# Strassen blocks of the last feed-forward layer: sums and the first two operand splits traced one block ahead; 24 general slots, 11 temporaries

## The chip, the cores and the metric

The kernel runs on one core of one Trainium2 chip. A core has TensorE (PE: matmuls, with the weight loads shown apart as PEld), VectorE (DVE), ScalarE (ACT), GpSimd (POOL) and SyncE (SP, which here only issues loads). The metric is the device time of one execution in microseconds (us). Lower is better. Before the change, three runs took 2473.5 to 2476.78 us, with a median of 2476.52.

## The reference

One inference step of a two-layer trunk on 512 prompt tokens and 8 sample tokens, 520 columns in all, with model width 1024. Each layer has two SwiGLU feed-forward blocks of inner width 2816; layer 0 has a gated MLP (gMLP) mixer, layer 1 an S5 state-space mixer; both have cross-attention into 256 memory tokens. The change touches the last feed-forward block of layer 1 alone (and two sizes that the whole program uses). What that block computes:

```python
def _swiglu(h, wg, wu, wd):
    return (jax.nn.silu(h @ wg) * (h @ wu)) @ wd
...
        x = x + 0.5 * _swiglu(_rmsnorm(x, norm_ffn2[i]), ffn2_wg[i], ffn2_wu[i], ffn2_wd[i])
    return _rmsnorm(x, norm_final), jnp.stack(new_re), jnp.stack(new_im), jnp.stack(new_v)
```

All of it is float32.

## The kernel before

Every float32 operand of a matmul is held as a high and a low half, and a product is three matmuls per 128 rows: high x high, high x low, low x high. A weight tile is split where it is used: ACT copies it to the reduced type (`wh`, L352), and VectorE subtracts that from the original (`wl`, L353). The pools of `wh` and of `wl` hold four tiles each (`WB = 4`), raw weights (`wr`) four (`WR = 4`).

The last feed-forward layer makes its 2816 hidden rows in 11 blocks of 256 columns of `wg` and `wu`. Blocks 0 and 1 are plain (`gu`). Blocks 2 to 10 go through `gu7`, which loads a block's weights as two tiles (`r1`, `r2`, four DMAs at L480) and runs `seven`: one level of a Strassen scheme, gate and up side by side. It splits the weights into quarters A11, A12, A21, A22 and the input into matching operands made once (`seven_x`: B11, B21, B22 and T4 lie in the tiles `xs`, T1 to T3 in `xt`). The seven products of a block and their weight operands, in the order of the program, are

- B11 with A11, then T2 with S2 = A21 + A22 - A11, then B21 with A12;
- T3 with S3 = A11 - A21, then T1 with S1 = A21 + A22;
- T4 with A22, then B22 with the second use of S2's tile, A12 - S2.

Each product is 24 matmuls of 260 columns (2 x 4 x 3). S1 and S2 are made by GpSimd (L368, L369), S3 and the second S2 by VectorE (L379, L380). The sums that combine products are VectorE's (L376 to L390, with one ACT copy at L374). Each of the four results goes through two scalings and a Silu (L485 to L487); when a hidden tile is complete it is split (L161 on ACT, L162 on VectorE).

After block 2, and then after each pair of blocks (3 and 4, 5 and 6, 7 and 8, 9 and 10), a down projection `down` takes four hidden tiles (192 matmuls) and adds to X (L500); the remaining two hidden tiles go through `last`. So blocks 4, 6, 8 and 10 follow directly on the block before them, and blocks 3, 5, 7 and 9 follow a down projection. "Odd" and "even" blocks below mean these.

S1, S2 and S3, hidden tiles, `xs`, `xt` and much else of the program are buffers of one size in one pool, the general slots (`SLOTS = 23`). Small float32 tiles of 520 columns (`t`: the sums e1 to e3, the block's halves of hidden rows, and in other stages the tiles of S5 and of its preparation) share a pool of 12.

What sets the order: the program is traced as Python, and when it is complete a planner of the framework lays down each engine's queue. It plays the program through once; of the instructions of an engine that are ready it takes the one traced first, and buffers of a pool are given out in the order in which their first writes were traced. On the chip the queues are fixed and each engine works through its own in order. Nothing in this layer is ordered by hand.

Of the kernel before, what the change touches and what calls it, by code (L numbers as in the profile page):

```python
# [9 lines left out]
F32 = mybir.dt.float32  # L10
F32R = mybir.dt.float32r
I32 = mybir.dt.int32
AF = mybir.ActivationFunctionType
# [10 lines left out]
DFF = 2816  # L24
# [5 lines left out]
KT = D // 128  # L30
NPAIR = 32
MAGIC = 12582912.0
SLOTS = 23
WB = 4
WR = 4
FFN_GROUPS = ((0, 6), (6, 12), (12, 18), (18, 22))
SEVEN_GROUPS = ((0, 4), (4, 8), (8, 12), (12, 16), (16, 20), (20, 22))
PLAIN = 2
BUFS = {"t": 12, "rs": 2, "rt": 4, "st": 10, "sti": 4, "mv": 4, "sc": 2, "cj": 2, "s5": 12, "s5i": 1,
        "s5r": 2}  # L40


class Prog:
    def __init__(self, ctx, tc, ins, outs, taps=None, stop=None):
# [4 lines left out]
        self.cp = ec(tc.tile_pool(name="cp", bufs=1))  # L49
        self.sp = ec(tc.tile_pool(name="sp", bufs=SLOTS))  # L50
        self.wp = ec(tc.tile_pool(name="wp", bufs=2))
# [15 lines left out]
    def tmp(self, shape=(128, NT), dt=F32, tag="t", name="t"):  # L67
        return self.tp.tile(list(shape), dt, name=self.nm(name), tag=tag, bufs=BUFS[tag])

    def ps(self):  # L70
        return self.pp.tile([128, 2, 512], F32, name=self.nm("ps"), tag="ps")
# [265 lines left out]

        return {"B11": B[0], "B21": B[2], "B22": B[3], "T1": T[0], "T2": T[1], "T3": T[2], "T4": B[1]}, last

    def seven(self, r1, r2, ops, ps):  # L340


        nc = self.nc
        V, G = nc.vector, nc.gpsimd
        sh = list(r1.shape[:3]) + [128]
        A11, A21, A12, A22 = r1[..., :128], r1[..., 128:], r2[..., :128], r2[..., 128:]
        n, nk = sh[1:3]

        def parts(src):
            hi = self.wp.tile(sh, F32R, name=self.nm("wh"), tag="wh", bufs=WB)  # L350
            lo = self.wp.tile(sh, F32R, name=self.nm("wl"), tag="wl", bufs=WB)
            nc.scalar.activation(hi, src, AF.Copy)  # L352
            V.tensor_sub(lo, src, hi.bitcast(F32))  # L353
            return hi, lo

        def product(p, w, b, first):

            hi, lo = w
            for x in range(n):
                for k in range(nk):  # L360
                    bh, bl = ops[b][k]
                    for i, (m, r) in enumerate(((hi, bh), (hi, bl), (lo, bh))):
                        self.mm(p[:, x, :HN], m[:, x, k], r, first and k == 0 and i == 0, k == nk - 1 and i == 2,
                                skip_group_check=not first)

        S1, S2, S3 = (self.slot(sh, F32, "S") for _ in range(3))
        w11 = parts(A11)
        G.tensor_add(S1, A21, A22)  # L368
        G.tensor_sub(S2, S1, A11)  # L369
        a, b, c = (ps() for _ in range(3))  # L370
        va, vb, vc = (p[:, :, :HN] for p in (a, b, c))
        e1, e2, e3 = (self.tmp([128, 2, HN]) for _ in range(3))
        product(a, w11, "B11", True)
        nc.scalar.copy(e1, va)  # L374
        product(b, parts(S2), "T2", True)
        V.tensor_add(e2, vb, e1)  # L376
        product(a, parts(A12), "B21", False)
        yield "11", va
        V.tensor_sub(S3, A11, A21)  # L379
        V.tensor_sub(S2, A12, S2)  # L380
        product(b, parts(S3), "T3", False)
        V.tensor_add(e3, vb, e1)
        product(c, parts(S1), "T1", True)
        V.tensor_add(e3, vc, e3)
        yield "22", e3
        product(b, parts(A22), "T4", False)
        V.tensor_add(e1, vb, e1)
        yield "21", e1
        product(c, parts(S2), "B22", False)
        V.tensor_add(e2, vc, e2)  # L390
        yield "12", e2


    def ffn(self, l, pre, fill=lambda: None, start=False, finish=None, seven=False):
        nc, ins = self.nc, self.ins
# [9 lines left out]
        rs = None  # L405
# [62 lines left out]

        ops, late = None, []

        def gu7(j):

            if late:
                late.pop()()
            cs = slice(j * 256, (j + 1) * 256)
            r = []
            for i in range(2):
                r.append(self.wp.tile([128, 2, 4, 256], F32, name=self.nm("wr"), tag="wr", bufs=WR))
                for x, w in enumerate((wg, wu)):
                    nc.sync.dma_start(r[i][:, x], w[i * 512 : (i + 1) * 512, cs].rearrange("(k p) m -> p k m", p=128))  # L480
            tw = [self.tmp() for _ in range(2)]
            for name, v in self.seven(*r, ops, self.ps):
                i, h = int(name[0]) - 1, int(name[1]) - 1
                d = self.tmp([128, 2, HN]) if name == "11" else v
                nc.vector.tensor_mul(d, v, rs[:, h : h + 1].to_broadcast([128, 2, HN]))  # L485
                nc.scalar.activation(d[:, 0], d[:, 0], AF.Silu)
                nc.vector.tensor_mul(tw[i][:, h * HN : (h + 1) * HN], d[:, 1], d[:, 0])  # L487
                if name in ("21", "12"):
                    hid[2 * j + i] = self.slot(name="hid")
                    self.split(hid[2 * j + i], tw[i])  # L490
            fill()

        def down(a, b):
            for q in range(4):
                w = self.wload(wd[a * 128 : b * 128, q * 256 : (q + 1) * 256], b - a, 256)
                for m in range(2):
                    p = self.ps()
                    self.lin(p, w[m], [hid[k] for k in range(a, b)])
                    xv = self.v2(self.X[:, 2 * q + m])
                    nc.vector.scalar_tensor_tensor(xv, p[:, :, :HN], 0.5, xv, op0=ALU.mult, op1=ALU.add)  # L500
            if b < DFF // 128:
                fill()
# [29 lines left out]
        done = 0  # L532
        for g0, g1 in SEVEN_GROUPS if seven else FFN_GROUPS:
            while done < min(DFF // 256, g1 // 2 + 1):
                (gu7 if seven and done >= PLAIN else gu)(done)
                done += 1
                if seven and done == 1:
                    ops, more = self.seven_x(key, xs)
                    late.append(more)
            if g1 == DFF // 128 and finish:  # L540
                last(g0, g1)
            else:
                down(g0, g1)
# [1056 lines left out]
```

## Time and profile before

| | |
|---|---|
| median of three runs | 2476.52 us |
| the profiled execution | 2482.79 us |
| its span, first to last instruction | 2481.1 us |
| mean granted TensorE clock | 0.985 |
| busy: PE / PEld / DVE / ACT / POOL | 2405.4 / 2328.3 / 1457.6 / 847.9 / 534.6 us |
| the last layer's blocks 2 to 10 and their down projections, 2131.5 to 2457 us | PE 312.37, DVE 244.15, ACT 125.25, POOL 61.45 us busy of 325.50 |

Busy time is the union of an engine's instructions. TensorE's is modelled at the ends, since its matmuls overlap. The granted clock is the share of TensorE's full clock that it was given: 1.00 is 2.4 GHz and 0.50 is 1.2 GHz.

### The profile page before, as it was taken

The numbers are of one execution on the slowest core, as the hardware profiler recorded it, in microseconds if no ns is written. First come the engines' busy times: TensorE is split into PE (matmuls) and PEld (weight loads), VectorE is DVE, ScalarE is ACT, GpSimd is POOL, SyncE is SP. The second block draws the span as 40 slices with busy tenths as digits, with TensorE's granted clock in tenths as the row PEclk, the third lists the DMA queues.
The fourth block names the chain that finished last, engine by engine and source line by source line (L and its number), as shares of the span: only waits on it lengthen the run. The fifth ranks groups of instructions, "written<-read, shape, count | busy, mean of one in ns | idle before, by whom it ended". The sixth has DMA issues, their size and how long they took to land.

```text
span 2481.1 us, 46658 instructions
## 1 busy us (share of the span) xinstructions
PE 2405.4 (97%) x19943; PEld 2328.3 (94%) x19943; DVE 1457.6 (59%) x2500; ACT 847.9 (34%) x1312; POOL 534.6 (22%) x511
## 2 busy tenths in 40 slices
PE   8999999999999999999999999999989999999998
PEld 7999999999999799999999999998779969999998
DVE  6534343648556656455556644536983645877775
ACT  4323232432224332233333423324432234433333
POOL 2111011102111011352532625201140101211221
PEclk8999999999999999999999999999999999999999
DMA  6243432421226622324333333324743462222221
GB/s 189 86 136 111 146 102 86 120 86 55 86 87 203 225 87 82 123 86 133 106 113 105 122 117 115 111 77 165 269 137 97 163 238 77 86 93 79 86 93 52
DMA packets 235661, 293.34 MB, mean 118 GB/s; under 512 B 7422, under 2 KB 203766, under 8 KB 235454
## 3 DMA queue, kind: packets, MB, share of 16 engines
q1 hardware_dynamic: 222247, 254.88, 31.9%
q10 hardware_dynamic: 12567, 34.38, 3.9%
q8 instruction: 157, 2.57, 0.4%
q0 software_dynamic: 640, 1.10, 0.2%
q14 instruction: 50, 0.41, 0.1%
HBM read 264.77 MB, written 25.56 MB: 117 GB/s over the span
## 4 chain that ended last, share of the span: by engine, by line
PE 85%; DVE 11%; issue 2%; ACT 2%; DMA 0%; POOL 0%; DVEq 0%; POOLq 0%; ACTq 0%
PE ps L77 83%; PE ps L80 1%; DVE wl L124 1%; DVE hid L162 1%; DVE ld L1350 1%; DVE sq L235 1%; DVE v L926 1%; DVE xs L292 0%; DVE t L686 0%; DVE wl L135 0%; DVE t L462 0%; ACT e L706 0%; DVE bi L1248 0%; DVE X L500 0%; DVE t L463 0%
## 5 line engine op out<-in xcount | busy, mean ns | idle before, releaser
L77 PE MATMUL ps<-xs,wh 128*128 128x260 f32 x6592 | 1088.1, 285 | 5.5 <-ACT xs L291 2.3
L77 PEld LDWEIGHTS ps<-xs,wh 128*128 128x128 f32 x6592 | 923.9, 190 | 10.4 <-ACT wh L352 3.2
L77 PE MATMUL ps<-xs,wl 128*128 128x260 f32 x3296 | 692.5, 284 | 0.2 <-POOL wl L124 0.2
L121 ACT ACTIVATE wh<-wr 128x1024 fp32r<-128x1024 f32 (+2 forms) x388 | 353.5, 913 | 960.7 <-PE ps L77 866.4
L77 PEld LDWEIGHTS ps<-xs,wl 128*128 128x128 f32 x3296 | 522.5, 190 | 0.4 <-POOL wl L124 0.4
L124 POOL TENSOR_TENSOR wl<-wr,wh 128x1024 fp32r<-128x1024 f32 (+2 forms) x94 | 196.8, 2094 | 1365.5 <-ACT wh L121 1350.4
L77 PE MATMUL ps<-hid,wh 128*128 128x260 f32 (+1 forms) x2816 | 456.3, 283 | 2.8 <-ACT hid L161 1.9
L77 PEld LDWEIGHTS ps<-hid,wh 128*128 128x128 f32 x2816 | 388.3, 189 | 4.7 <-ACT hid L161 2.3
L124 DVE TENSOR_TENSOR wl<-wr,wh 128x1024 fp32r<-128x1024 f32 (+2 forms) x294 | 327.1, 1115 | 89.0 <-ACT wh L121 87.6
L77 PE MATMUL ps<-hid,wl 128*128 128x260 f32 (+2 forms) x1408 | 286.0, 283 | 0.0
L77 PEld LDWEIGHTS ps<-hid,wl 128*128 128x128 f32 x1408 | 218.5, 188 | 0.0
L500 DVE SCALAR_TENSOR_TENSOR X<-ps,X 128x520 f32<-128x520 f32 x136 | 94.9, 698 | 184.1 <-PE ps L77 183.8
L462 DVE TENSOR_TENSOR t<-ps,rs 128x520 f32<-128x520 f32 x70 | 48.9, 698 | 184.9 <-PE ps L77 184.9
L460 DVE TENSOR_TENSOR t<-ps,rs 128x520 f32<-128x520 f32 x70 | 48.8, 697 | 136.3 <-PE ps L77 105.4
L162 DVE TENSOR_TENSOR hid<-t,hid 128x520 fp32r<-128x520 f32 x88 | 87.1, 990 | 29.9 <-ACT hid L161 29.4
L77 PE MATMUL ps<-xt,wh 128*128 128x260 f32 x432 | 86.3, 300 | 10.2 <-ACT wh L352 10.2
L161 ACT ACTIVATE hid<-t 128x520 fp32r<-128x520 f32 x88 | 56.2, 638 | 114.6 <-DVE t L463 108.0
L77 PE MATMUL ps<-o,wh 128*128 128x260 f32 x512 | 92.5, 290 | 1.6 <-DVE o L162 1.0
L77 PE MATMUL ps<-z,wh 128*128 128x260 f32 x512 | 85.8, 290 | 1.5 <-ACT t L1378 1.0
L77 PEld LDWEIGHTS ps<-xt,wh 128*128 128x128 f32 x432 | 72.4, 204 | 11.3 <-ACT wh L352 11.3
L77 PEld LDWEIGHTS ps<-o,wh 128*128 128x128 f32 x512 | 74.6, 188 | 8.4 <-DVE o L162 3.4
L77 PE MATMUL ps<-um,wh 128*128 128x260 f32 x512 | 82.4, 283 | 0.0
(352 smaller groups left out, 2926.2 us busy)
## 6 DMA issues: line engine op xcount, KB each, us to landing
wr<-in_ffn_wg SPq DMA_DIRECT2D x34, 1024.0 KB, 5.4
wr<-in_ffn_wu SPq DMA_DIRECT2D x34, 1024.0 KB, 5.5
wr<-in_ffn_wd SPq DMA_DIRECT2D x36, 768.0 KB, 4.3
wr<-in_ffn_wd SPq DMA_DIRECT2D x32, 512.0 KB, 3.4
wr<-in_a_w_in SPq DMA_DIRECT2D x16, 1024.0 KB, 5.5
kc<-in_cache_mem_k SPq DMA_DIRECT2D x32, 512.0 KB, 7.3
vc<-in_cache_mem_v SPq DMA_DIRECT2D x32, 512.0 KB, 7.5
wr<-in_ffn_wg SPq DMA_DIRECT2D x20, 512.0 KB, 4.0
```

The source lines that it names most:

```text
L77: self.nc.tensor.matmul(out, lhsT=lhsT, rhs=rhs, start=start, stop=stop, **kw)
L80: self.nc.tensor.transpose(out, in_, self.ident[base : base + k, base : base + k])
L121: nc.scalar.activation(hi, r, AF.Copy)
L124: eng.tensor_sub(lo, r, hi.bitcast(F32))
L161: nc.scalar.activation(sl[:, 0, n0:n1], src, AF.Copy)
L162: nc.vector.tensor_sub(sl[:, 1, n0:n1], src, sl.bitcast(F32)[:, 0, n0:n1])
L235: (nc.gpsimd if k == 7 and early or k < 4 and not early else nc.vector).tensor_add(sums[-1], sums[-1], t)
L460: nc.vector.tensor_mul(self.v2(t), pg[:, :, :HN], rs)
L462: nc.vector.tensor_mul(self.v2(w), pu[:, :, :HN], rs)
L500: nc.vector.scalar_tensor_tensor(xv, p[:, :, :HN], 0.5, xv, op0=ALU.mult, op1=ALU.add)
L926: V_.tensor_scalar(vt[q][:, :, c], vt[q][:, :, c], mv[:, c, 0:1], rl[:, c : c + 1], op0=ALU.subtract, op1=ALU.mult)
L1350: V.tensor_tensor_scan(w, self.mag4[:, 4 * i + a : 4 * i + a + 1].to_broadcast([128, 128]), w, 0.0, op0=ALU.mult, op1=ALU.add)
```

## The change

`seven` is cut in two. `seven_begin` makes S1 and S2 and the splits of A11 and S2, and `begin7` loads the block's weights and calls it. For an odd block `begin7` is called in the last quarter of the down projection before it; for an even block from within the block before it, behind the product T4 (`ahead`). Block 2 calls it at its own start. Inside `seven`, the splits of A12, of S3, and of A22 and the second S2 are traced somewhat earlier than the products and results that they used to follow, and the second S2 behind the sum e3. The general slots grow from 23 to 24 and the temporaries shrink from 12 to 11, for the whole program.

```diff
-SLOTS = 23
+SLOTS = 24
...
-BUFS = {"t": 12, "rs": 2, "rt": 4, "st": 10, "sti": 4, "mv": 4, "sc": 2, "cj": 2, "s5": 12, "s5i": 1,
+BUFS = {"t": 11, "rs": 2, "rt": 4, "st": 10, "sti": 4, "mv": 4, "sc": 2, "cj": 2, "s5": 12, "s5i": 1,
...
+    def seven_begin(self, r1, r2):
+
+        sh = list(r1.shape[:3]) + [128]
+        A11, A21, A22 = r1[..., :128], r1[..., 128:], r2[..., 128:]
+        S1, S2 = (self.slot(sh, F32, "S") for _ in range(2))
+        self.nc.gpsimd.tensor_add(S1, A21, A22)
+        self.nc.gpsimd.tensor_sub(S2, S1, A11)
+        return r1, r2, S1, S2, self.seven_parts(A11), self.seven_parts(S2)
...
-        S1, S2, S3 = (self.slot(sh, F32, "S") for _ in range(3))
-        w11 = parts(A11)
-        G.tensor_add(S1, A21, A22)
-        G.tensor_sub(S2, S1, A11)
+        S3 = self.slot(sh, F32, "S")
...
         product(a, w11, "B11", True)
         nc.scalar.copy(e1, va)
-        product(b, parts(S2), "T2", True)
+        product(b, w2, "T2", True)
         V.tensor_add(e2, vb, e1)
-        product(a, parts(A12), "B21", False)
+        w12 = parts(A12)
+        V.tensor_sub(S3, A11, A21)
+        w3 = parts(S3)
+        product(a, w12, "B21", False)
         yield "11", va
-        V.tensor_sub(S3, A11, A21)
+        product(b, w3, "T3", False)
+        V.tensor_add(e3, vb, e1)
+        w1 = parts(S1)
         V.tensor_sub(S2, A12, S2)
-        product(b, parts(S3), "T3", False)
-        V.tensor_add(e3, vb, e1)
-        product(c, parts(S1), "T1", True)
+        product(c, w1, "T1", True)
         V.tensor_add(e3, vc, e3)
+        w22, w4 = parts(A22), parts(S2)
         yield "22", e3
-        product(b, parts(A22), "T4", False)
+        product(b, w22, "T4", False)
+        ahead()
         V.tensor_add(e1, vb, e1)
         yield "21", e1
-        product(c, parts(S2), "B22", False)
+        product(c, w4, "B22", False)
...
+        def begin7(j):
+            if j in begun or j >= DFF // 256:
+                return
             if late:
                 late.pop()()
...
+            begun[j] = self.seven_begin(*r)
+
+        def gu7(j):
+
+            begin7(j)
+            ahead = lambda: j % 2 == 1 and begin7(j + 1)
             tw = [self.tmp() for _ in range(2)]
-            for name, v in self.seven(*r, ops, self.ps):
+            for name, v in self.seven(begun.pop(j), ops, ahead):
...
                 w = self.wload(wd[a * 128 : b * 128, q * 256 : (q + 1) * 256], b - a, 256)
+                if q == 3 and seven and PLAIN <= done < DFF // 256:
+                    begin7(done)
```

## Rows read from the trace of the kernel before

**Rows 1.** The page: busy us (share of the span) xinstructions of each engine.

```profile
PE 2405.4 (97%) x19943; PEld 2328.3 (94%) x19943; DVE 1457.6 (59%) x2500; ACT 847.9 (34%) x1312; POOL 534.6 (22%) x511
```

**Rows 2.** Waits of TensorE, 2030 us on: us in total, times, longest us.

```profile
PE ps L77 <- ACT wh L352: 12.4, 10, 2.1
```

**Rows 3.** Timeline of TensorE, block 4: start, us, instruction [idle before <- releaser].

```profile
2198.75 0.28 PE L77 MATMUL ps<-xs,wl 128*128 128x260 f32 x1
2201.18 0.51 PE L77 MATMUL ps<-xt,wh 128*128 128x260 f32 x2 [2.14 <-ACT wh L352]
...
2209.64 0.40 PE L77 MATMUL ps<-xt,wh 128*128 128x260 f32 x2
```

**Rows 4.** Timeline of TensorE, block 3: first matmuls of T2 and of T3.

```profile
2178.70 0.40 PE L77 MATMUL ps<-xt,wh 128*128 128x260 f32 x2
...
2184.47 0.40 PE L77 MATMUL ps<-xt,wh 128*128 128x260 f32 x2
```

**Rows 5.** Windows, block 4: A:B us, busy us (xinstructions) by engine, PEclk, DMA, GB/s.

```profile
2203.70:2207.00 3.30, 3.30 (x18) 3.30 (x17) 2.40 (x3) 0.27 (x1) 0.00 (x0) 0.50 0.29 100
```

**Rows 6.** Timeline of TensorE: blocks 2 (two rows) and 10.

```profile
2131.34 0.28 PE L77 MATMUL ps<-xs,wl 128*128 128x260 f32 x1
...
2141.42 0.40 PE L77 MATMUL ps<-xt,wh 128*128 128x260 f32 x2
...
2403.78 0.28 PE L77 MATMUL ps<-xs,wl 128*128 128x260 f32 x1
```

**Rows 7.** Timeline of GpSimd, block 4: the sum S2.

```profile
2177.86 3.27 POOL L369 TENSOR_TENSOR S<-S,wr 128x1024 f32<-128x1024 f32 x1
```

**Rows 8.** Timeline of VectorE, end of block 3 and start of block 4.

```profile
2190.44 0.70 DVE L384 TENSOR_TENSOR t<-ps,t 128x520 f32<-128x520 f32 x1 [0.64 <-PE ps L77]
...
2198.59 0.43 DVE L487 TENSOR_TENSOR t<-t 128x260 f32<-128x260 f32 x1 [0.49 <-ACT t L486]
...
2200.34 1.22 DVE L379 TENSOR_TENSOR S<-wr 128x1024 f32<-128x1024 f32 x1
...
2204.88 1.22 DVE L353 TENSOR_TENSOR wl<-S,wh 128x1024 fp32r<-128x1024 f32 x1
```

**Rows 9.** Timeline of ACT, blocks 3 and 4.

```profile
2170.12 1.06 ACT L352 ACTIVATE wh<-S 128x1024 fp32r<-128x1024 f32 x1 [1.85 <-PE ps L77]
...
2191.91 0.42 ACT L486 ACTIVATE t<-t 128x260 f32<-128x260 f32 x1 [3.36 <-DVE t L485]
...
2199.59 0.57 ACT L374 COPY t<-ps 128x520 f32<-128x520 f32 x1
2200.07 1.06 ACT L352 ACTIVATE wh<-S 128x1024 fp32r<-128x1024 f32 x1
2201.03 1.05 ACT L352 ACTIVATE wh<-wr 128x1024 fp32r<-128x1024 f32 x1
```

**Rows 10.** Windows: block 3 from T2 to block 4's B11; rest of block 4.

```profile
2176.00:2199.00 23.00, 23.00 (x193) 22.82 (x191) 16.91 (x20) 7.87 (x11) 5.06 (x2) 1.00 0.08 25
2199.00:2221.20 22.20, 19.50 (x146) 19.05 (x146) 17.42 (x23) 10.19 (x14) 0.00 (x0) 0.92 0.29 91
```

**Rows 11.** Waits in the gMLP stage, 575 to 612 us.

```profile
ACT wh L121 <- POOL lnb L947: 7.4, 1, 7.4
...
PE ps L77 <- DVE t L912: 4.8, 1, 4.8
```

**Rows 12.** Waits of VectorE over the whole span.

```profile
DVE t L460 <- POOL M L1196: 30.5, 4, 7.6
```

**Rows 13.** Timelines of GpSimd and VectorE in the S5 stage, one turn.

```profile
1762.99 0.10 POOL L1354 MEMSET t<- 128x4 f32 x1 [3.47 <-PE ps L77]
...
1766.26 0.12 POOL L1296 MEMSET t<- 128x24 f32 x1 [3.02 <-PE ps L77]
...
1772.78 0.11 POOL L1354 MEMSET t<- 128x4 f32 x1 [6.36 <-DVE z L162]
...
1773.24 1.38 DVE L1298 SCALAR_TENSOR_TENSOR t<-X,gains,rs 128x512 f32<-128x512 f32 x1
```

More of the change, by code (lines that the diff above doesn't have):

```diff
@@ L338, in seven_x, with seven_parts, seven @@
         return {"B11": B[0], "B21": B[2], "B22": B[3], "T1": T[0], "T2": T[1], "T3": T[2], "T4": B[1]}, last
-    def seven(self, r1, r2, ops, ps):
+    def seven_parts(self, src):
+        sh = list(src.shape)
+        hi = self.wp.tile(sh, F32R, name=self.nm("wh"), tag="wh", bufs=WB)
+        lo = self.wp.tile(sh, F32R, name=self.nm("wl"), tag="wl", bufs=WB)
+        self.nc.scalar.activation(hi, src, AF.Copy)
+        self.nc.vector.tensor_sub(lo, src, hi.bitcast(F32))
+        return hi, lo
+    def seven_begin(self, r1, r2):
[5 more added lines that the diff above has]
+        return r1, r2, S1, S2, self.seven_parts(A11), self.seven_parts(S2)
+    def seven(self, begun, ops, ahead):
         nc = self.nc
-        V, G = nc.vector, nc.gpsimd
-        sh = list(r1.shape[:3]) + [128]
+        V = nc.vector
+        r1, r2, S1, S2, w11, w2 = begun
+        sh = list(S1.shape)
         A11, A21, A12, A22 = r1[..., :128], r1[..., 128:], r2[..., :128], r2[..., 128:]
         n, nk = sh[1:3]
[L349 to L354, printed above, removed]
+        parts = self.seven_parts
         def product(p, w, b, first):
@@ L364, in product @@
                                 skip_group_check=not first)
-        S1, S2, S3 = (self.slot(sh, F32, "S") for _ in range(3))
-        w11 = parts(A11)
-        G.tensor_add(S1, A21, A22)
-        G.tensor_sub(S2, S1, A11)
-        a, b, c = (ps() for _ in range(3))
+        S3 = self.slot(sh, F32, "S")
+        a, b, c = (self.ps() for _ in range(3))
         va, vb, vc = (p[:, :, :HN] for p in (a, b, c))
@@ L469, in ffn @@
         ops, late = None, []
-        def gu7(j):
+        begun = {}
+        def begin7(j):
+            if j in begun or j >= DFF // 256:
+                return
             if late:
```

## Prediction, made before the changed kernel was run

> **What bounds the kernel now.** I read the page's busy times first: TensorE is busy for 97% of the span [rows 1], so little but its idle time and its slow clock can be won. The changed code runs only in the last feed-forward layer, so I then listed what TensorE waits for from 2030 us to the end. One line leads: 10 waits, 12.4 us, all for ACT's weight split at L352 [rows 2]. The timeline shows where they sit. In block 4, the last matmul of product B11 starts at 2198.75; TensorE then idles 2.14 us ahead of T2's first pair, and the product T3 starts only at 2209.64 [rows 3]. In block 3 the same two products, T2 and B21, run from 2178.70 to 2184.47: 5.77 us for 48 matmuls, 0.12 each [rows 4]. So block 4's T2 was due at 2198.75 + 0.12 = 2198.87, and the two products took 10.77 us. The difference, 5.00 us, is what one stall costs. Part of it is clock: behind the stall, 18 matmuls filled 3.30 us at a granted clock of 0.50, the 1.2 GHz level [rows 5].
>
> There are five such stalls (two waits each), in blocks 2, 4, 6, 8 and 10. Blocks 4 to 10 repeat one pattern: B11's last matmul of block 10 starts at 2403.78 [rows 6], three pairs of blocks behind block 4's, 68.34 us a pair. Block 2 is a little cheaper: 2131.34 + 0.12 to 2141.42 is 9.96 [rows 6], so 4.19 over. The odd blocks have none.
>
> **Why block 4 stalls.** T2 needs the split of S2. GpSimd finished S2 at 2177.86 + 3.27 = 2181.13 [rows 7]. The four split buffers go round by product, so this split takes the one that T1, four products earlier, gives back: near 2190.4 (VectorE's L384 reads T1's result at 2190.44) [rows 8]. Yet ACT makes this split at 2200.07, directly behind the copy L374 of the same block, although it had idled 3.36 us ahead of 2191.91 [rows 9]. So neither data nor a buffer held it; its place in ACT's queue did. What follows it says the same: the split of A12, whose load GpSimd had already read for S1, ahead of S2, comes at 2201.03, and VectorE's S3 at 2200.34 stands behind block 3's last hidden tile [rows 8, 9]. In the trace order of the program all of this begins behind block 3's last store, and the planner hands out buffers in that order. In odd blocks a down projection lies between, so the queue has run ahead: S2's split of block 3 is at 2170.12, 8.6 us ahead of its product at 2178.70 [rows 4, 9].
>
> **The change, part by part.** *Even blocks 4, 6, 8, 10.* S1, S2 and the splits of A11 and S2 are now traced in the middle of the odd block before, ahead of its two hidden tiles. S2's tile no longer queues behind them, so its split can be planned for the moment when T1 frees a buffer, 2190.4, and end near 2191.5; its VectorE half (1.22 us) ends near 2193. T2 is due at 2198.87: 6 us to spare. Removed: 5.00 us in each of four blocks. The work itself stays: the same seven split pairs, two GpSimd sums, two VectorE sums and four loads per block.
>
> *What is late next.* A12's split needs the buffer that T4 frees at 2190.4 + 2.9 = 2193.3 (24 matmuls of 0.12 later); it is due at 2198.87 + 2.88 = 2201.75 and has time. S3 is the tight one: it is still traced behind block 3's hidden tiles. It can start when VectorE's L487 ends, 2198.59 + 0.43 = 2199.02 [rows 8]. Sum 1.22, split 1.06, lower half 1.22 and two hops of some 0.1 give 2202.7; from its present start, 2200.34, 2204.0. T3 is due at 2198.87 + 5.77 = 2204.64, and first reads the lower half at 2204.88. That is 0.8 to 2.2 us of slack, so I take no stall.
>
> *VectorE's room.* In the 22.20 us from 2199 it is busy 17.42 [rows 10]; without the stall the stretch is 17.2 us. But S2's and A12's halves (2.4 us) go into the 23.00 us before it, which has 16.91 busy [rows 10]. That leaves 15.0 of 17.2 and 19.3 of 23.0: dense, not full.
>
> *The queues passed.* On ACT the two pulled splits (1.06 us each) pass block 3's last Silus and hidden splits and L374; on VectorE their halves pass L387 to L162. These may be a microsecond later; who waits is the next down projection, a whole block (20 us) away. The four loads stay in their order on SP: behind the last load of the down projection for odd blocks, with nothing between for even ones. On GpSimd the sums pass nothing. The splits hold the same 4 + 4 buffers in the same order as now.
>
> *Odd blocks 3, 5, 7, 9 and the new order inside a block.* Their start moves into the down projection's last quarter, but they have no stall to lose [rows 4]: 0. Tracing A12, S3 and their splits ahead of B21, and S2's second use behind the third sum, changes no dependence; S2's second split has two products (5.8 us) of slack: 0.
>
> *Block 2* still starts behind block 1's last hidden tile; its 4.19 us stay. Bounds 0 to -4.19.
>
> *24 slots* reach the whole program. The one place in the rows where a slot is waited for elsewhere is the gMLP stage: ACT stands 7.4 us for GpSimd's L947, which frees a gain tile. TensorE's 4.8 us stall there waits for VectorE's L912 [rows 11], not ACT, so I take 0. Bounds: the whole stall and a slow-clock loss of 1.65 like the one above (half of 3.30 us) go, -6.5; one more VectorE split (0.67) in front of L912, +0.7.
>
> *11 temporaries.* Reuse moves one release earlier in the ring. In the preparation of S5, VectorE's L460 already waits 7.6 us four times for GpSimd to free a temporary [rows 12]. TensorE's list of waits has no line for it, so: 0. If the wait grew as the ring shrinks (7.6 x 12 / 11, 0.7 more) and nothing covered it, +2.8. In the S5 stage each turn takes five temporaries. GpSimd clears the next u4 at 1766.26; with one fewer it would have to wait for the release seen at 1772.78; VectorE first writes u4 at 1773.24 [rows 13]. That fits, barely: 0. The upper bound is in the rivals.
>
> **Sum.** The profiled execution takes 2482.79 us (span 2481.1 and 1.7 around it). 2482.79 - 4 x 5.00 = 2462.8. The median of the runs shown is 2476.52, 6.3 less than the profiled one; the saving is TensorE time in either: 2456.5.
>
> **Rivals.**
> *Stall at S3 instead.* If VectorE and ACT keep their present order behind L162, S3's lower half comes third in the burst, as at 2204.88 to 2206.10 now; T3 waits from 2204.88 (its third matmul) to 2206.1, 1.2 us, and with a slow stretch of 1.65 after it, 2.9. Four times: 4.8 to 11.4 of the 20 come back, 2461 to 2468. For it: VectorE is dense and S3 keeps its place. Against it: the burst is shorter by two splits.
> *Nothing moves.* If the four split buffers are the limit, earlier tracing changes no queue: 2476.5. For it: most ACT splits in the odd block wait for TensorE to free one [rows 9]. Against it: the stalled split did not. The Trainium skill, "Perfetto Trace Analysis", section "Optimization Strategy", says that one gap repeating on the engine that should be full can mean too few buffers for the next tile. By that reading the ring of four, which the change leaves, keeps the stall and the time is 2476.5. This trace does not bear it out: the buffer was free 9.6 us before the split.
> *More goes.* Block 2's stall goes too: 2452.3. Or the gMLP stall does: 2450.
> *Slower: a temporary short in S5.* Place: the eight turns of the S5 stage, where VectorE is the chain. If the 12th temporary was what let GpSimd clear tiles ahead of it, each turn waits as GpSimd does at its second clear, 3.47 us [rows 13]: 27.8, and 2476.5 - 20 + 27.8 = 2484.3. It decides from 20 / 8 = 2.5 us a turn. For it: these clears do wait for releases. Against it: the tightest use, u4's, still fits.
>
> **How the numbers follow.** Forecast 0.65, more goes 0.08, stall at S3 0.14, nothing 0.07, S5 0.06. The likeliest is 2456.5. The range takes in the second and third: 2449 (2450 and a microsecond of scatter) to 2469 (2468 and one). About 0.2%, 5 us, is what a measurement can tell from no change: faster 0.87, same 0.07, slower 0.06.
>
> **What would show it.** In the changed trace S2's split of blocks 4, 6, 8, 10 stands ahead of L374 on ACT, T2 to T3 takes 5.8 us there, the clock stays at 1.00 behind it, and a pair with its down projection takes 63.3 us in place of 68.3. Block 2 keeps its stall. I am wrong if the split still follows L374, if T3 starts late by what T2 gained, or if the S5 turns grow.

## The result: 2456.3 us, and the profile after

The changed kernel takes 2456.34 us (median of 4 runs, 2454.60 to 2457.83), the kernel before 2476.65 in the same comparison: a ratio of 0.992, 95% interval 0.9902 to 0.9937. A second comparison, on another occasion, gave 2457.21 against 2478.20: 0.991, 0.9893 to 0.9927. The prediction was 2456.5.

The list of TensorE's waits from 2030 us on answers to [rows 2]; its columns are us in total, times, longest:

```profile
PE ps L77 <- ACT wh L344: 2.1, 2, 1.6
PE ps L77 <- DVE sq L1502: 1.9, 1, 1.9
```

(The splits of the seven products, L352 before, are now L344.) Ten waits and 12.4 us have become two waits and 2.1 us. TensorE's timeline says which two are left. Block 2, as in [rows 6]:

```profile
2122.44 0.28 PE L77 MATMUL ps<-xs,wl 128*128 128x260 f32 x1
...
2124.36 0.51 PE L77 MATMUL ps<-xt,wh 128*128 128x260 f32 x2 [1.64 <-ACT wh L344]
...
2125.31 0.78 PE L77 MATMUL ps<-xs,wh 128*128 128x260 f32 x2 [0.44 <-ACT wh L344]
```

And the first matmuls of T4 in block 3 and of T2, B21 and T3 in block 4, as in [rows 3], with T2 of blocks 6, 8 and 10 behind them:

```profile
2181.41 0.40 PE L77 MATMUL ps<-xs,wh 128*128 128x260 f32 x2
...
2190.01 0.40 PE L77 MATMUL ps<-xt,wh 128*128 128x260 f32 x2
...
2192.91 0.40 PE L77 MATMUL ps<-xs,wh 128*128 128x260 f32 x2
...
2195.78 0.40 PE L77 MATMUL ps<-xt,wh 128*128 128x260 f32 x2
...
2253.09 0.40 PE L77 MATMUL ps<-xt,wh 128*128 128x260 f32 x2
...
2316.22 0.40 PE L77 MATMUL ps<-xt,wh 128*128 128x260 f32 x2
...
2379.56 0.40 PE L77 MATMUL ps<-xt,wh 128*128 128x260 f32 x2
```

T2 and B21 of block 4 take 2195.78 - 2190.01 = 5.77 us, as they do in an odd block [rows 4], and none of these rows has an idle time. From T2 to T2 a pair of blocks takes 63.08, 63.13 and 63.34 us, where it took 68.34. The windows that answer to [rows 5] and [rows 10] (block 3 from T2's neighbourhood to block 4's B11, then block 4) show VectorE fuller and the clock at its higher level, 2.4 GHz, throughout:

```profile
2167.20:2190.00 22.80, 22.80 (x192) 22.80 (x192) 19.83 (x23) 9.92 (x13) 3.24 (x1) 1.00 0.08 25
2190.00:2207.20 17.20, 17.20 (x146) 17.20 (x145) 14.29 (x21) 8.36 (x13) 0.00 (x0) 1.00 0.37 115
```

ACT, as in [rows 9]: S2's split for block 4, then the copy of its B11, then S3's split together with S1's:

```profile
2181.57 1.06 ACT L344 ACTIVATE wh<-S 128x1024 fp32r<-128x1024 f32 x1 [1.86 <-PE ps L77]
...
2190.21 0.59 ACT L383 COPY t<-ps 128x520 f32<-128x520 f32 x1 [0.19 <-PE ps L77]
...
2191.92 2.01 ACT L344 ACTIVATE wh<-S 128x1024 fp32r<-128x1024 f32 x2 [0.56 <-DVE S L387]
```

The split that stood behind the copy now stands 8.6 us ahead of it, and what releases it is TensorE, which gives back a split buffer.

### The profile page after: what moved, and what is told of

The parts are those of the page before. It is cut to its first block, busy times and chain, and to the rows that moved or that the text cites. A ratio compares the mean times of both kernels' runs of the same rounds, so it can differ in the third digit from the quotient of the medians.

```text
span 2452.9 us, 46675 instructions
## 1 busy us (share of the span) xinstructions
PE 2386.8 (97%) x19943; PEld 2312.7 (94%) x19943; DVE 1456.5 (59%) x2500; ACT 849.0 (35%) x1312; POOL 526.5 (21%) x511
## 5 line engine op out<-in xcount | busy, mean ns | idle before, releaser
L77 PE MATMUL ps<-xt,wh 128*128 128x260 f32 x432 | 79.9, 285 | 1.6 <-ACT wh L344 1.6
L235 POOL TENSOR_TENSOR sq<-sq,sq 128x520 f32<-128x520 f32 x22 | 32.8, 1492 | 217.4 <-ACT sq L231 216.8
```

What stands on the lines that cost most here:

```text
L77: self.nc.tensor.matmul(out, lhsT=lhsT, rhs=rhs, start=start, stop=stop, **kw)
L235: (nc.gpsimd if k == 7 and early or k < 4 and not early else nc.vector).tensor_add(sums[-1], sums[-1], t)
```

## The experiments

Theory: an even block's S2 split is late because the planner hands out general slots in trace order. When it plays the program through, S1 and S2 get theirs only behind the hidden tiles of the block before, so it lays down S2's split behind them too. On the chip the sum itself was not late: GpSimd had finished it at 2181.13 [rows 7], 18.9 us ahead of its split at 2200.07 [rows 9]. No run shows the planner's play itself, only the queues that come of it. Rivals: the ring of four split buffers holds the split; the split itself must be traced ahead; the new order inside a block, or the sizes, make the gain. Ratios are against the kernel before, run beside each experiment.

**A ring of their own for the sums, nothing traced elsewhere** (an edit of the kernel before).

```diff
-SLOTS = 23
+SLOTS = 21
...
-BUFS = {"t": 12, ...
+BUFS = {"t": 11, ...
...
-        S1, S2, S3 = (self.slot(sh, F32, "S") for _ in range(3))
+        S1, S2, S3 = (self.sp.tile(sh, F32, name=self.nm("S"), tag="S", bufs=3) for _ in range(3))
```

> The kernel before with one edit that moves nothing in the trace order: the three sum tiles S1, S2, S3 come from a ring of their own (three buffers) in place of the general slots, of which 21 are left; 11 temporaries make room. If the stall comes from the general slots being handed out in trace order (S1 of an even block behind the last hidden tile of the block before), S2's split now goes ahead of the copy of B11, the four stalls go, and the time is 2476.6 - 20 = 2456.6, with up to some 3 us on top where two general slots fewer are missed in other stages. If the ring of four split buffers holds the split, or if the split must itself be traced ahead, the stalls stay: 2476.6 or a little above.

Measured: 2459.17 us, ratio 0.9924 (0.9902 to 0.9946). TensorE's waits from 2030 to 2420 us begin:

```profile
PE ps L77 <- DVE dg L273: 3.7, 1, 3.7
PE ps L77 <- DMA vc<-in_cache_mem_v: 2.2, 2, 1.6
```

No wait for a split is left, not even block 2's, which stays in the changed kernel. What the run loses again are the two waits shown, at 2094 and 2034 us, ahead of these blocks. With the same four split buffers and the same trace order, the stall is gone: the ring of four is refuted. On ACT of this run S2's split of block 4 comes before the copy L374:

```profile
2188.49 1.06 ACT L352 ACTIVATE wh<-S 128x1024 fp32r<-128x1024 f32 x1 [1.54 <-PE ps L77]
...
2198.07 0.57 ACT L374 COPY t<-ps 128x520 f32<-128x520 f32 x1
```

GpSimd's S2 of that block comes no earlier than before:

```profile
2180.04 2.41 POOL L369 TENSOR_TENSOR S<-S,wr 128x1024 f32<-128x1024 f32 x1 [1.23 <-DVE wl L353]
```

It ends at 2182.45, where it ended at 2181.13. So on the chip the sum came no earlier; what moved is the place of its split in ACT's queue.

**Only loads and sums ahead** (an edit of the changed kernel).

```diff
-        return r1, r2, S1, S2, self.seven_parts(A11), self.seven_parts(S2)
+        return r1, r2, S1, S2
...
-        r1, r2, S1, S2, w11, w2 = begun
+        r1, r2, S1, S2 = begun
...
         parts = self.seven_parts
+        w11, w2 = parts(r1[..., :128]), parts(S2)
```

> The changed kernel, but of the work begun ahead only the four loads and the sums S1 and S2 stay ahead; the splits of A11 and S2 are traced at the start of their own block again, behind the hidden tiles of the block before. If it is the handing out of S1's slot that kept the split back, the planner puts the split at the same place as in the changed kernel: 2456.3, pair of blocks 63.3 us. If the splits' own place in the trace is what counts, S2's split stands behind the copy of B11 again and the stalls return: 2476.

Measured: 2456.78 us, 0.9901 (0.9872 to 0.9931); TensorE waits for splits only in block 2, with the same 2.1 us. The splits need not be traced ahead. Where the sums take general slots, it is enough that the loads and the sums are; the run with the own ring, which moves no load, shows that the loads' place does not decide.

**One half of the early start at a time** (edits of the changed kernel).

```diff
-            ahead = lambda: j % 2 == 1 and begin7(j + 1)
+            ahead = lambda: None
```

> The changed kernel without the early start of even blocks; odd blocks are still begun in the down projection's last quarter, and the new order inside a block, 24 slots and 11 temporaries stay. By the prediction only the even blocks' early start is worth anything: five stalls are back, 2476.3. If the new order inside a block or the odd blocks' early start is what helped, the time stays near 2456; if they share, something between.

Measured: 2475.53 us, 0.999 (0.9978 to 1.0002), and TensorE's waits from 2030 us on are those of before:

```profile
PE ps L77 <- ACT wh L344: 12.5, 10, 2.2
```

The other half:

```diff
-                if q == 3 and seven and PLAIN <= done < DFF // 256:
-                    begin7(done)
```

> The changed kernel without the early start of odd blocks in the down projection; even blocks are still begun one block ahead. By the prediction the odd part is worth 0: 2456.3, odd blocks with T2 and B21 in 5.8 us as before. If the odd blocks' splits now come late behind the down projection's (the new order inside a block needs them earlier), four odd blocks stall by 1 to 5 us: 2460 to 2476.

Measured: 2453.85 us, 0.9902 (0.9881 to 0.9923), with the same two waits as the changed kernel. So the even blocks' early start is the whole gain; the odd blocks' is worth nothing that these runs can tell, and neither is the new order inside a block, which the run with the own ring does without.

**The two sizes alone, and the change without them.**

```diff
-SLOTS = 23
+SLOTS = 24
...
-BUFS = {"t": 12, ...
+BUFS = {"t": 11, ...
```

> The kernel before with 24 general slots and 11 temporaries and no other edit. By the prediction the two sizes are worth 0: 2476.6, five stalls as before, the wait of some 4.5 to 4.8 us in the gMLP stage still there. If the 24th slot lets S1 be handed out earlier, the stalls shrink: down to 2457. If 11 temporaries cost something in S5 or its preparation: 2477 to 2480.

Measured: 2476.85 us, 0.9989 (0.9975 to 1.0003), ten waits and 12.5 us for the splits. In the other direction, the changed kernel with 23 and 12:

> The changed kernel with the old sizes, 23 general slots and 12 temporaries. If the tracing alone makes the gain, 2456.6 and only block 2's stall left. If the early sums need the 24th slot, S1 and S2 of the even blocks get theirs only when the down projection has freed hidden tiles; that is still a whole block ahead, so 2456 to 2458; should they be later than the stalled split was, stalls come back, up to 2476.

Measured: 2458.27 us, 0.9924 (0.9905 to 0.9943), two waits and 2.1 us. Neither size is needed for the gain, nor does either cost anything that shows.

**Ten temporaries** (the changed kernel with one fewer again, `"t": 10`).

> The changed kernel with 10 temporaries in place of 11; nothing else. In the changed kernel's S5 stage GpSimd clears the next u4 at 1771.09, 0.4 us ahead of VectorE's first write at 1771.49; the next release of a temporary there is the one that it waits for at 1774.34. If the ring is that close to short, each clear now waits for that later release and VectorE stands some 2.9 to 3.3 us in each of the eight turns: 23 to 26 us, 2479 to 2483. If the turn has room behind VectorE or the ring is not the limit, 2456 to 2460.

Measured: 2453.54 us, 0.9903 (0.9882 to 0.9924): no loss, and the expectation was wrong. It had set a clear against the write of another tile. There are eight u4, and so eight such clears on GpSimd and eight first writes on VectorE, each laid down in the order of the program. Counted so, the clear at 1771.09 is the seventh and the write at 1771.49 the sixth. The seventh clear and the seventh write, first in the changed kernel, then with ten:

```profile
1771.09 0.12 POOL L1320 MEMSET t<- 128x24 f32 x1 [9.54 <-DVE z L162]
...
1785.55 1.19 DVE L1322 SCALAR_TENSOR_TENSOR t<-X,gains,rs 128x512 f32<-128x512 f32 x1
```

```profile
1771.97 0.12 POOL L1320 MEMSET t<- 128x24 f32 x1 [12.24 <-PE ps L77]
...
1783.27 1.12 DVE L1322 SCALAR_TENSOR_TENSOR t<-X,gains,rs 128x512 f32<-128x512 f32 x1
```

With 11 the clear comes 14.46 us ahead of its tile's first write, with ten 11.30 us. In the kernel before, by the same count, it comes 21.06 us ahead, at 1766.26 [rows 13] for this write:

```profile
1787.32 1.17 DVE L1298 SCALAR_TENSOR_TENSOR t<-X,gains,rs 128x512 f32<-128x512 f32 x1
```

So each temporary fewer brings the clear nearer to its use, and with ten there is still room: VectorE waits for no clear. How few temporaries would cost time was not tested.

**S3 made late** in blocks 4, 6, 8 and 10 (the result is the same).

```diff
-        V.tensor_sub(S3, A11, A21)
+        for _ in range(4 if late else 1):
+            V.tensor_sub(S3, A11, A21)
```

(`late` is true for these four blocks.)

> The changed kernel with VectorE's sum S3 done four times instead of once in blocks 4, 6, 8 and 10 (three repeats of 1.22 us; the result is the same). In the changed kernel S3's lower half ends at 2194.24 and is first read at 2196.02, 1.8 us of slack, and with the repeats two short operations of VectorE also come ahead of it: the lower half would end near 2198.5. If S3 is next in line as predicted, T3 waits some 2 to 2.5 us in each of four blocks, with 0 to 1.65 us of slow clock behind it: 8 to 17 us, 2464 to 2473. If something else decides T3's start, 2456.

Measured: 2473.32 us, 0.9978 (0.9968 to 0.9987), just past the upper end. TensorE's waits from 2140 to 2420 us:

```profile
PE ps L77 <- ACT wh L344: 7.4, 4, 1.8
PE ps L77 <- DVE wl L345: 3.0, 4, 0.8
```

T3 waits in each of the four blocks, first for S3's split, then for its lower half: 2.6 us a block. With one repeat (`2 if late`):

> The changed kernel with one repeat of VectorE's sum S3 (1.22 us) in blocks 4, 6, 8 and 10, where the run with three repeats stalled T3 by 1.84 us and 0.75 us a block. S3's lower half has 1.8 us of slack, one repeat takes 1.22 and the short sum of T2 comes ahead of it for another 0.6: it uses the slack up, so no stall or one of a few tenths: 2456 to 2459. If the stall with three repeats came from VectorE being short over the whole block, a third of the loss should show: 2462.

Measured: 2453.79 us, 0.99 (0.9879 to 0.9921), and its list has no wait for L345 and no more for L344 than the two of block 2. The loss begins between one and three repeats: it is a slack that runs out, not VectorE's load over the block.

**Block 2 begun early too** (an edit of the changed kernel). Its loads, sums and splits are traced in the second plain block; the operand splits that overwrite what the plain block reads keep their place.

```diff
                 if m or pre is None:
                     ...
+                if seven and j == PLAIN - 1 and m == 1:
+                    begin7(PLAIN)
                 t, w = self.tmp(), self.tmp()
...
             if j in begun or j >= DFF // 256:
                 return
-            if late:
-                late.pop()()
...
             begin7(j)
+            if late:
+                late.pop()()
```

> The changed kernel with block 2 begun early as well: its loads, sums and two splits are traced in the second plain block, ahead of that block's last hidden tile. If slots handed out in trace order are the cause of block 2's stall as of the others, it goes: 2456.3 - 4.2 = 2452.1, and TensorE's list of waits has none for the splits of the seven products. If block 2 stalls for something else (operand sums made just ahead of it on ACT and VectorE), 2456.

> The changed kernel as it is, beside the kernel that begins block 2 early: 2456.3. It gives the reference for that comparison and shows how far two executions of one program differ stage by stage.

Measured: 2451.31 us, 0.9887 (0.9872 to 0.9902), beside 2457.21 for the changed kernel. That is 5.9 us less where 4.2 was expected; the two intervals just overlap, so the size is uncertain. The four runs, 2448.05 to 2452.62, all lie below the changed kernel's four, 2452.89 to 2458.88, and the trace is plain. TensorE's waits from 2030 to 2420 us now begin at half a microsecond:

```profile
PE ps L80 <- ACT t L829: 0.5, 1, 0.5
```

## Why the prediction was right, step by step

*The stall's price and count.* Four stalls of 5.00 us were to go. The medians differ by 20.3 us (the interval makes it 16 to 24), and the pair of blocks became 63.1 to 63.3 us long where 63.3 was foreseen. That the median came within 0.2 us of the forecast is luck: kernels whose last layer shows the same two waits had medians from 2453.54 to 2458.27.

*Queue, not data or ring.* Right, and the experiments sharpen it. The prediction laid the stall to the split's place in ACT's queue and to the trace order by which buffers are handed out. The runs with the own ring and with only the sums ahead point to which handing out it is: that of the sums' general slots, in the planner's play. The Trainium skill ("Perfetto Trace Analysis", section "Optimization Strategy") says that a gap which keeps repeating can mean that there is not room enough for the next tile. That was not so here: a 24th slot alone left all ten waits (12.5 us), and 21 slots with a ring of three beside them, 24 buffers again and the same 11 temporaries, left none. What counted was the order in which buffers were handed out, not their number.

*When the split can come.* The forecast was the moment when T1 frees its buffer, 2190.4 in the time of the kernel before, where T4 follows T1. In the changed trace, which is 8.9 us earlier there, T4 starts at 2181.41 and the split at 2181.57.

*S3 next, with 0.8 to 2.2 us of slack.* It is next, and the slack is 1.8 us. VectorE's sum, block 3's last hidden split and S3's lower half, and then the first matmul of T3 that reads that half:

```profile
2190.61 1.22 DVE L387 TENSOR_TENSOR S<-wr 128x1024 f32<-128x1024 f32 x1
2191.75 0.69 DVE L162 TENSOR_TENSOR hid<-t,hid 128x520 fp32r<-128x520 f32 x1
2193.02 1.22 DVE L345 TENSOR_TENSOR wl<-S,wh 128x1024 fp32r<-128x1024 f32 x1 [0.58 <-ACT wh L344]
```

```profile
2196.01 0.28 PE L77 MATMUL ps<-xt,wl 128*128 128x260 f32 x1
```

The lower half ends at 2194.24. The prediction's lower end had S3 stay behind the last hidden split on VectorE; it goes 1.1 us ahead of it, which is the case of the upper end. The two runs with repeats confirm the place: 1.22 us more cost nothing, 3.66 us brought back a stall of 2.6 us a block.

*VectorE's room.* 15.0 of 17.2 and 19.3 of 23.0 us were foreseen; 14.29 of 17.20 and 19.83 of 22.80 came.

*Block 2.* It kept its stall as said, and for the reason said: begun early, it loses it.

*24 slots at 0.* Right in the sum. ACT's 7.4 us for the gain tile [rows 11] are gone, in the run with the two sizes alone too, and TensorE's stall there hardly moves:

```profile
PE ps L77 <- DVE t L936: 4.5, 1, 4.5
```

*11 temporaries at 0.* Right in the sum, wrong in one of its reasons. The wait of [rows 12] grew from 30.5 to 32.0 us, and TensorE's list still has no line for it:

```profile
DVE t L473 <- POOL M L1220: 32.0, 4, 8.0
```

u4's clear did move to the next release, as worked out from [rows 13]. But "that fits, barely" was a misreading: it set the seventh clear against the sixth write. Against its own write the clear has 14.46 us to spare, not 0.40. The rival of a temporary short in S5 and the expectation of the run with ten stood on the same slip, so the forecast of 0 was safer than the prediction knew.

*The profiled executions.* Here the prediction's own sum, 2462.8 us for the profiled execution, does not meet the profiled one after, 2454.6: they lie 28.2 us apart, not 20. The last matmul of block 2's B11, ahead of any stall that the change removes, starts at 2122.44 after and at 2131.34 before [rows 6], so 8.9 us of it arose earlier. The changed kernel's second profile tells what that is worth. The same stretch of the same program, first in one execution and then in the other (the third number from the end is the granted clock):

```profile
1835.00:1843.00 8.00, 6.10 (x113) 5.57 (x114) 3.61 (x6) 1.47 (x4) 0.00 (x0) 1.00 0.01 2
```

```profile
1835.00:1843.00 8.00, 6.69 (x75) 5.81 (x79) 3.03 (x6) 0.40 (x2) 0.00 (x0) 0.57 0.01 2
```

The second execution's span is 2456.7 us, the first one's 2452.9, and it reaches the same matmul of block 2 later by 3.85 us:

```profile
2126.29 0.28 PE L77 MATMUL ps<-xs,wl 128*128 128x260 f32 x1
```

From that matmul to the end the first takes 330.5 and the second 330.4 us; the kernel before takes 2481.1 - 2131.34 = 349.8. So the part that the change touches gained 19.3 us in the profiles, close to the 20.0 of the sum. The 8.9 us ahead of it are no more than executions of one program differ by: thirteen runs of the kernel before, in one comparison, took 2473.44 to 2484.00 us. Whether any of them is the change's own was not separated. The prediction had carried the saving over to the median, and there it came out.

*The slow stretch at 1.65.* The prediction's bounds took half of a slow stretch of 3.30 us as its cost. The run with S3 made late shows 1.5 us (last section). It stands only in rivals and bounds, so the forecast does not hang on it.

## What to carry to other kernels

If an engine's instruction runs late although its data and its own buffer are ready, look at the order in which its inputs' tiles were asked for. Where a planner hands out buffers in program order and writes the queues from that, one tile asked for behind a late one puts all that follows from it late in the queues, even if on the chip the tile is ready in time. Asking for the tile earlier, or giving it a ring of its own, can help where more buffers do not. And price a stall with what comes behind it, the slow clock among it: here the idle time of the five stalls, 12.4 us [rows 2], was about half of the 4 x 5.00 + 4.19 = 24.2 us that they cost.

## What the runs showed of the hardware

A stall does not always bring a slow clock. With S3 made late, blocks 4 and 6 had the same idle time at T3, 1.84 and 0.75 us against 1.85 and 0.75; behind block 4's the granted clock stayed at 1.00 (2.4 GHz), behind block 6's it was 0.72 over the window, so part of it ran at the 1.2 GHz level (behind blocks 8 and 10 it was 0.72 over six microseconds too):

```profile
2200.00:2206.00 6.00, 4.63 (x36) 4.42 (x37) 5.43 (x7) 4.37 (x6) 0.00 (x0) 1.00 0.33 94
2267.00:2273.00 6.00, 5.25 (x30) 5.04 (x31) 5.23 (x6) 3.50 (x5) 0.00 (x0) 0.72 0.46 141
```

What the slow part cost can be read from the first and the last matmul of T3 that use the lower half, in block 4 and then in block 6:

```profile
2201.88 0.39 PE L77 MATMUL ps<-xt,wl 128*128 128x260 f32 x1 [0.75 <-DVE wl L345]
...
2204.51 0.28 PE L77 MATMUL ps<-xt,wl 128*128 128x260 f32 x1
...
2268.10 0.58 PE L77 MATMUL ps<-xt,wl 128*128 128x260 f32 x1 [0.75 <-DVE wl L345]
...
2272.24 0.29 PE L77 MATMUL ps<-xt,wl 128*128 128x260 f32 x1
```

From the one to the other it takes 2.63 us in block 4 and 4.14 us in block 6: 1.5 us more for the same matmuls. So in this run the price of one stall is its idle time plus either nothing or about 1.5 us; the four stalls cost (2473.32 - 2457.21) / 4 = 4.0 us each on average.
